# Five arms for an expert: nested comparisons become one switch with a hint, and gather, one-hot turn and add-back leave the arms

## The chip, the core and the metric

One core of one Trainium2 chip. The time is the device time of one execution in microseconds (us). TensorE is called PE, VectorE DVE, ScalarE ACT, GpSimd POOL and SyncE SP; each engine runs its own instruction stream, and semaphores order them. A "hw" matmul is one record in the trace: a float32 product of two passes shows as two.

## What is computed

Two layers of a diffusion trunk over 256 latent tokens of 1024 channels. The last part of the second layer is the one that the change touches, a SwiGLU of eight experts of which each token takes two:

```python
logits = h @ router_w + router_b
top_logit, top_idx = lax.top_k(logits, 2)
gates = einsum('btk,btke->bte', softmax(top_logit), one_hot(top_idx, 8))
for e in range(8):
    y = y + gates[..., e:e + 1] * (silu(h @ w1[e]) * (h @ w3[e])) @ w2[e]   # inner width 1408
```

The residual, a LayerNorm and the store follow.

## The kernel before

The mixers, the dense SwiGLU and the router come first; they order their instructions with a planner and by hand, and the change leaves that order as it was. Then the experts run one after the other, e = 0 to 7.

How many tokens an expert has is known only at run time. The counts are summed on TensorE (L1640), copied to int32 (`cnt`, L1644) and read into registers of PE, DVE, ACT and SP by `nc.values_load` (L1689). For each expert the function `pick` (L1934) halves the five possible arms by nested `tc.If(vals[e] > bound)` (L1940): up to 32 tokens the arm Tiny, up to 64 Small, up to 128 Full, up to 192 Full and Small, else two Fulls. Each of the four engines branches for itself. In the instruction streams the arms stand in the order Full+Full, Full+Small, Full, Small, Tiny; a comparison that holds goes on with what follows, one that doesn't jumps, and an arm ends in a jump over those behind it (Tiny, the last, has none behind it). POOL is in none of the arms.

The weights of an expert are 17 pieces of up to 1 MB; 19 slots hold them, and after its use each slot is loaded with the piece that is 19 further on (`pload`, issued by SP inside the arm).

An arm multiplies its tokens by the pieces in the order "u0 u1 u2 d0 u3 d1 u4 d2 u5 d3 t5 d4 d5" (u: up, d: down, t5: the turn of the last inner chunk). In a Full arm the weights are split on ACT (`wh`, L1286) and DVE (`wl`, L1287) into two parts that TensorE multiplies in three products (`mm3`, L248). Three further steps lie inside the arm of expert e:

- `gather` (L1656) of expert e + 1, at t5: 16 products pick its tokens with a one-hot matrix `oh` (L1663), and ACT and DVE modulate them in turn into `xg` (L1648, L1650).
- `turn_oh` (L1667), right behind it: two transposes of `oh` and a copy on ACT, kept for the way back.
- `scatter` (L1710) of expert e - 1, behind u1: four products with `yf` (L1713) and four additions on DVE into the sum (L1715).

In an arm with two blocks scatter comes first, a second one-hot and gather for the second block follow, and `turn_oh` closes the arm. `end` (Tiny: L1764, Full: L1855) leaves the expert's result in `yf`. The one-hot of expert e + 1 is made by POOL ahead of the branch (L1654).

## Time and profile before

| what | value |
|---|---|
| time, median of 3 runs | 1463.27 us (1457.28 to 1464.77) |
| the profiled execution: span from first to last instruction | 1468.2 us; no other time of it is given |
| busy: PE, weight loads, DVE, ACT, POOL | 1187.8, 895.5, 876.3, 645.8, 421.1 us |
| mean granted TensorE clock | 0.905 of full |
| HBM | 273.17 MB read, 195 GB/s over the span |

Busy times are sums over stages with different limits. The stage of the change runs from the router at 951 us to the end of the eighth expert at 1449 us.

### The profile page before, as it was taken

The page shows a single profiled execution, that of the slowest core. Times are in us where ns is not written, and L with a number is a line of the kernel's source. Part 1 is how long each engine was busy: PE and PEld are TensorE (multiplying, and loading weights), DVE is VectorE, ACT ScalarE, POOL GpSimd, SP SyncE. Part 2 cuts the span into 40 slices and gives each one's busy share as a digit, 9 for nine tenths or more (in the row PEclk, how much of TensorE's full clock was granted, in tenths as well). Part 3 has the DMA queues.
Part 4 walks back from the last instruction along what each step waited for, and adds up shares of the span by engine and source line. Part 5 has one row for each costly group of instructions (what it writes and reads, how often), then busy time and mean ns, then how long its engine had stood idle before and what let it go on. Part 6 is the DMA issues. An engine that isn't in the chain of part 4 may idle for free.

```text
span 1468.2 us, 26379 instructions
## 1 busy us (share of the span) xinstructions
PE 1187.8 (81%) x10101; PEld 895.5 (61%) x10101; DVE 876.3 (60%) x1632; ACT 645.8 (44%) x1426; POOL 421.1 (29%) x653
## 2 busy tenths in 40 slices
PE   1589679998797989878799989658978999548946
PEld 0266458776575666544698988545856556335843
DVE  7897226447566865345877785805867456113924
ACT  3433135567665766321344444214757344003810
POOL 6242122647856775501622230400000000000000
PEclk7799789999888999999899999879989999779978
DMA  8324736646555655658445555469968345589920
GB/s 342 108 79 175 224 114 205 181 122 164 141 129 117 149 147 142 133 168 337 167 170 172 175 180 202 175 243 415 370 213 289 116 150 198 205 330 412 390 83 30
DMA packets 139661, 288.59 MB, mean 197 GB/s; under 512 B 64432, under 2 KB 91184, under 8 KB 116272
## 3 DMA queue, kind: packets, MB, share of 16 engines
q1 hardware_dynamic: 136128, 278.50, 55.9%
q10 hardware_dynamic: 3312, 7.31, 1.4%
q8 instruction: 119, 1.95, 0.6%
q14 instruction: 102, 0.84, 0.2%
HBM read 273.17 MB, written 12.60 MB: 195 GB/s over the span
## 4 chain that ended last, share of the span: by engine, by line
PE 37%; issue 5%; DVE 4%; DMA 3%; ACT 1%; POOL 0%; DVEq 0%; ACTq 0%; POOLq 0%
PE pb L248 23%; PE pb L1740 3%; PE pb L1713 2%; PE pb L1663 2%; PE pb L1775 2%; DMA slot<-in_moe_w_dram 2%; DMA arena<-in_moe_w_dram 1%; PE pb L1819 1%; PE pb L1758 1%; PE pb L1789 1%; DVE wl L1287 1%; ACT wh L1286 1%; DVE usl L1435 0%; PE pb L1578 0%; DMA arena<-in_lnrows_dram 0%
## 5 line engine op out<-in xcount | busy, mean ns | idle before, releaser
L1287 DVE TENSOR_TENSOR wl<-arena,wh 128x512 fp32r<-128x512 f32 x262 | 214.5, 838 | 76.6 <-ACT wh L1286 74.4
L1286 ACT ACTIVATE wh<-arena 128x512 fp32r<-128x512 f32 x262 | 160.9, 629 | 123.4 <-PE pb L248 114.9
L1654 POOL TENSOR_SCALAR oh<-consts,consts 128x128 f32<-128x128 f32 x14 | 8.7, 633 | 381.3 <-PE pb L1758 133.5
L954 POOL TENSOR_TENSOR arena<-arena 128x126 f32<-128x126 f32 (+22 forms) x248 | 110.0, 444 | 19.4
L248 PE MATMUL pb<-usl,wh 128*128 128x256 f32 x352 | 101.5, 289 | 5.6 <-DVE usl L1435 5.6
L248 PE MATMUL pb<-ush,wh 128*128 128x256 f32 x352 | 101.6, 291 | 1.8 <-DVE fsg L1453 1.8
L248 PE MATMUL pb<-ush,wl 128*128 128x256 f32 x352 | 101.0, 288 | 0.0
L1286 ACT ACTIVATE wh<-slot 128x512 fp32r<-128x512 f32 x122 | 75.1, 629 | 39.8 <-PE pb L248 35.8
L1287 DVE TENSOR_TENSOR wl<-slot,wh 128x512 fp32r<-128x512 f32 x122 | 80.9, 688 | 18.7 <-ACT wh L1286 17.9
L266 PE MATMUL pb<-arena,sct 128*32 128x256 f32 x448 | 70.3, 424 | 23.4 <-DMA arena<-in_ada_w_dram 23.2
L1748 DVE TENSOR_TENSOR mh<-mh,pb 64x128 f32<-64x128 f32 (+1 forms) x24 | 7.0, 291 | 134.0 <-ACT mh L1747 108.7
L1317 POOL TENSOR_TENSOR arena<-arena,rows 128x2048 f32<-128x2048 f32 x11 | 51.5, 4685 | 104.9 <-DMA arena<-in_ffn_w_dram 104.9
L1099 DVE SCALAR_TENSOR_TENSOR sv<-sv,wc,pb 64x64 f32<-64x64 f32 x192 | 45.8, 278 | 57.4 <-PE pb L1083 22.2
L952 POOL TENSOR_TENSOR arena<-arena 128x126 f32<-128x126 f32 (+22 forms) x124 | 62.8, 507 | 51.3 <-DMA arena<-s 42.2
L248 PEld LDWEIGHTS pb<-usl,wh 128*128 128x128 f32 x352 | 69.2, 197 | 8.9 <-DVE usl L1435 6.5
L248 PE MATMUL pb<-wh,xsh 128*128 128x512 f32 (+1 forms) x180 | 71.7, 398 | 0.0
L248 PEld LDWEIGHTS pb<-ush,wh 128*128 128x128 f32 x352 | 68.8, 197 | 4.4 <-DVE fsg L1453 2.0
L248 PE MATMUL pb<-wl,xsh 128*128 128x512 f32 (+1 forms) x180 | 71.3, 396 | 0.0
L248 PEld LDWEIGHTS pb<-ush,wl 128*128 128x128 f32 x352 | 69.1, 197 | 1.2
L952 POOL TENSOR_TENSOR arena<-arena,X 128x126 f32<-128x126 f32 (+22 forms) x124 | 57.6, 464 | 39.4 <-DMA X<-s 30.6
L248 PE MATMUL pb<-wh,xsl 128*128 128x512 f32 (+1 forms) x180 | 67.6, 375 | 0.0
L1074 ACT ACTIVATE sv<-pb 64x128 f32<-64x128 f32 x128 | 34.6, 270 | 68.3 <-PE pb L1068 55.5
(441 smaller groups left out, 3100.9 us busy)
## 6 DMA issues: line engine op xcount, KB each, us to landing
slot<-in_moe_w_dram SPq DMA_DIRECT2D x62, 1024.0 KB, 7.9
arena<-in_moe_w_dram SPq DMA_DIRECT2D x58, 1024.0 KB, 8.0
arena<-in_ffn_w_dram SPq DMA_DIRECT2D x33, 1024.0 KB, 5.1
arena<-in_ada_w_dram SPq DMA_DIRECT2D x112, 256.0 KB, 3.1
hvr<-in_w_rkv_dram SPq DMA_DIRECT2D x12, 1024.0 KB, 5.9
wr<-in_ada_w_dram SPq DMA_DIRECT2D x10, 1024.0 KB, 6.0
sv<-v_d SPq DMA_DIRECT2D x128, 64.0 KB, 2.7
arena<-k_d SPq DMA_DIRECT2D x8, 640.0 KB, 4.0
```

The source lines that it names most:

```text
L248: i = nc.tensor.matmul(ps, lhsT=a[x], rhs=b[y], start=start and n == 0, stop=stop and n == 2)
L266: nc.tensor.matmul(ps[64 * h + 32 * g:64 * h + 32 * g + 32, 0:256], lhsT=sct[:, k], rhs=w[:, 256 * g:256 * g + 256], start=(k == 0), stop= ...
L952: eng.tensor_tensor(mv, T[:, cs, j:j + 1].to_broadcast([P, nci, nii]), X[:, ii, j].unsqueeze(1).to_broadcast([P, nci, nii]), op=ALU.mult)
L954: eng.tensor_tensor(T[:, cs, ii], T[:, cs, ii], mv, op=ALU.subtract)
L1074: nc.scalar.activation(sv_(si, d, 1)[zd(d)], PB[6][zd(d), 0:128], AF.Copy, scale=-1.0)
L1099: nc.vector.scalar_tensor_tensor(t[:, x], sv_(si, d, 0)[zd(d), x], wc_b[wc.i][zd(d), h, si:si + 1], PB[6][zd(d), 128 + 64 * h:192 + 64 * h ...
L1286: nc.scalar.activation(hi, r[:, o:o + PART], AF.Copy)
L1287: nc.vector.tensor_tensor(lo, r[:, o:o + PART], hi, op=ALU.subtract)
L1317: S.behind(nc.gpsimd.tensor_tensor(w, w, gt.unsqueeze(1).to_broadcast(w.shape), op=ALU.mult))
L1663: nc.tensor.matmul(pt[:, P * j:P * j + n], lhsT=z[:, t, P * dt:P * dt + P], rhs=oh[:, t, 0:n], start=(t == 0), stop=(t == 1))
L1713: nc.tensor.matmul(ps, lhsT=ohT[:, t], rhs=yf[:, 512 * j:512 * j + 512], start=True, stop=True)
L1740: nc.tensor.matmul(ps[32 * g:32 * g + 32, 0:P], lhsT=xg[:, k, 0:32], rhs=m[g], start=(k == 0), stop=(k == DT - 1))
```

## The change

The counts are no longer copied. Four comparisons on DVE with 32, 64, 128 and 192 add up to the number of the arm, 0 to 4, and that is loaded into the registers. `pick` and its `tc.If` are gone: `tc.Switch` jumps to one of five arms by that number, in the order Tiny, Small, Full, Full+Small, Full+Full. `tc.switch_hint` stands ahead, and the switch puts a hint for the jump at an arm's end at the start of each arm. `gather`, `turn_oh` and `scatter` stand between two switches instead of inside the arms, for experts 1 to 7 (the first gather and the last scatter lay outside the arms already). Comments and docstrings are gone too, and lines behind the top of the file move by one to seven.

```diff
+BOUNDS = (32, 64, 128, 192)
...
     cnt = c2p.tile([P, NE], I32, name="cnt")
-    S.chain(nc.vector.tensor_copy(cnt, pc[:, 0:8]))
+    armf = c2p.tile([P, NE], F32, name="armf")
+    S.chain(nc.vector.tensor_scalar(armf, pc[:, 0:8], float(BOUNDS[0]), None, op0=ALU.is_gt))
+    for i, b in enumerate(BOUNDS[1:]):
+        S.chain(nc.vector.scalar_tensor_tensor(armf if i + 2 < len(BOUNDS) else cnt, pc[:, 0:8], float(b), armf,
+                                               op0=ALU.is_gt, op1=ALU.add))
...
-    vals = [nc.values_load(cnt[0:1, e:e + 1], engines=(ENG.PE, ENG.DVE, ENG.Activation, ENG.SP), min_val=0, max_val=256)
-            for e in range(NE)]
+    ARM_ENGINES = (ENG.PE, ENG.DVE, ENG.Activation, ENG.SP)
+    vals = [nc.values_load(cnt[0:1, e:e + 1], engines=ARM_ENGINES, min_val=0, max_val=len(BOUNDS)) for e in range(NE)]
...
         if two:
-            if e > 0:
-                scatter(e - 1, ohT[(e - 1) % 2])
             onehot(e, 1, nc.vector, ohB)
...
-            if (a, c) == ("u", 1) and e > 0 and not two:
-                scatter(e - 1, ohT[(e - 1) % 2])
-            if a == "t" and not end:
-                gather(oh, xgs[0])
-                if not two:
-                    turn_oh(oh, ohT[(e + 1) % 2])
         if two:
             bl[1].end()
             scatter(e, ohT[(e + 1) % 2])
-            if not end:
-                turn_oh(oh, ohT[(e + 1) % 2])
         bl[0].end()
...
-    def pick(e, lo, hi):
...
-        m = (lo + hi) // 2
-        with tc.If(vals[e] > ARMS[m][0]) as c:
-            pick(e, m + 1, hi)
-        with c.Else():
-            pick(e, lo, m)
...
     for e in range(NE):
+
+        tc.switch_hint({g: vals[e] for g in ARM_ENGINES}, len(ARMS), f"arm{e}")
+        if e > 0:
+            gather(oh, xgs[0])
+            turn_oh(oh, ohT[e % 2])
+            scatter(e - 1, ohT[(e - 1) % 2])
         if e + 1 < NE:
             onehot(e + 1, 0, nc.gpsimd, oh)
-        pick(e, 0, len(ARMS) - 1)
+        for k in tc.Switch({g: vals[e] for g in ARM_ENGINES}, len(ARMS), hint=f"arm{e}"):
+            arm(e, ARMS[k])
```

How this stands in the built program is seen in the instruction order of two engines. First TensorE between the gather of expert 0 and its arm; TENSOR_LOAD reads a register, ISA calculates with registers. Before:

```order
L1663 MATMUL pb_64<-oh,z_8444 128x128 x7
L1663 MATMUL pb_69<-oh,z_8444 128x128 x7
L1671 MATMUL pb_70<-consts,oh 128x128
L1689 TENSOR_LOAD cnt
L1940 COMPARE_AND_BRANCH x2
```

After, with the triples of experts 2 to 6 left out:

```order
L1669 MATMUL pb_69<-oh,z_8444 128x128 x7
L1677 MATMUL pb_70<-consts,oh 128x128
L1696 TENSOR_LOAD cnt
L1936 ISA
L1936 BRANCH_PREFETCH_HINT
...
L1696 TENSOR_LOAD cnt
L1936 ISA
L1936 BRANCH_PREFETCH_HINT
L2080 SWITCH_STRIDE
L2080 ISA x2
L1943 BRANCH_PREFETCH_HINT
L1746 MATMUL pb_63<-arena,xg 32x128 x32
```

All eight register loads and all eight hints that the loop writes for the eight switches stand ahead of the first switch; DVE, ACT and SP have theirs at the same place. The hint of L1943 is the first instruction of an arm and belongs to the jump at its end. Before, each expert's load stood ahead of its own comparisons.

Second, TensorE between the last arm of expert 0 and the first of expert 1. Before, with the end of the Tiny arm, in which gather and turn stand among the last products:

```order
L1663 MATMUL pb_69<-oh,z_8444 128x128 x8
L1752 MATMUL pb_64<-consts,mh 128x32
L1663 MATMUL pb_70<-oh,z_8444 128x128 x8
L1671 MATMUL pb_63<-consts,oh 128x128 x2
L1758 MATMUL pb_65<-slot_8732,small 32x256 x8
L1758 MATMUL pb_65<-slot_8734,consts 32x256 x4
L1940 UNCONDITIONAL_BRANCH
L1689 TENSOR_LOAD cnt
L1940 COMPARE_AND_BRANCH x2
```

After, with the end of the last arm in the stream:

```order
L249 MATMUL pb_66<-wh,hh1l 128x512
L2080 UNCONDITIONAL_BRANCH
L1677 MATMUL pb_63<-consts,oh 128x128 x2
L1669 MATMUL pb_70<-oh,z_8444 128x128 x8
L1669 MATMUL pb_69<-oh,z_8444 128x128 x8
L1719 MATMUL pb_64<-yf,consts 128x512
L1719 MATMUL pb_63<-yf,consts 128x512
L1719 MATMUL pb_70<-yf,consts 128x512
L1719 MATMUL pb_69<-yf,consts 128x512
L2080 SWITCH_STRIDE
L2080 ISA x2
L1943 BRANCH_PREFETCH_HINT
```

Turn, gather and the four products of the add-back now stand in a row between the jump out of one arm and the jump into the next. DVE has the same place like this after the change:

```order
L1861 TENSOR_TENSOR yf<-pb_65,gt 128x512
L1861 TENSOR_TENSOR yf<-pb_66,gt 128x512
L2080 UNCONDITIONAL_BRANCH
L1656 TENSOR_SCALAR xg<-pb_70,raa,rab 128x128 x2
L1656 TENSOR_SCALAR xg<-pb_69,raa,rab 128x128
L1721 SCALAR_TENSOR_TENSOR x_8519<-pb_64,consts,x_8519 128x512
L1656 TENSOR_SCALAR xg<-pb_69,raa,rab 128x128
L1721 SCALAR_TENSOR_TENSOR x_8519<-pb_63,consts,x_8519 128x512
L1721 SCALAR_TENSOR_TENSOR x_8519<-pb_70,consts,x_8519 128x512
L1721 SCALAR_TENSOR_TENSOR x_8519<-pb_69,consts,x_8519 128x512
L2080 SWITCH_STRIDE
L2080 ISA x2
```

DVE reaches its own switch only behind the last of the four additions, which waits for the last product of the add-back. On all engines what stands ahead of the router and behind the last expert keeps its order.

## Rows read from the trace of the kernel before

**Rows 1.** The page's first part (busy time of each engine) and, of its second part, the granted TensorE clock in 40 slices of 36.7 us.
```profile
PE 1187.8 (81%) x10101; PEld 895.5 (61%) x10101; DVE 876.3 (60%) x1632; ACT 645.8 (44%) x1426; POOL 421.1 (29%) x653
PEclk7799789999888999999899999879989999779978
```

**Rows 2.** The waits of TensorE from 950 us to the end: which line waited, for what by the profile, us in total, times, longest. "issue" is time in which the engine waited for nothing that the profile shows.
```profile
PE pb L1740 <- issue: 54.4, 6, 17.4
PE pb L1740 <- DMA arena<-in_moe_w_dram: 20.1, 1, 20.1
PE pb L1819 <- issue: 11.2, 2, 5.7
PE pb L1819 <- DVE xsl L1804: 8.8, 1, 8.8
PE pb L1713 <- issue: 7.6, 1, 7.6
```

**Rows 3.** TensorE in the eight stretches between the last product ahead of an expert's arm and the first product in it, experts 0 to 7 in order: stretch in us, its length, PE busy (products), granted clock, mean busy share of the DMA engines, GB/s. The last row is the sum of their lengths.
```profile
960.20:974.50 14.30, 0.00 (x0) 0.68 0.53 189
1001.10:1006.50 5.40, 0.00 (x0) 0.99 1.01 405
1063.80:1072.50 8.70, 0.00 (x0) 0.73 0.35 122
1130.90:1138.40 7.50, 0.00 (x0) 0.84 0.39 142
1246.80:1264.10 17.30, 0.00 (x0) 0.65 0.18 60
1293.80:1313.70 19.90, 0.00 (x0) 0.57 0.87 338
1341.20:1346.80 5.60, 0.00 (x0) 0.78 1.02 414
1404.60:1421.40 16.80, 0.00 (x0) 0.63 0.12 37
sum 95.50, PE 0.00; mean PE 0.00
```

**Rows 4.** The line of the comparisons (L1940) on TensorE's sequencer: first all of its records, then those around each of the eight stretches of rows 3 in the same order: count, lowest, median and highest duration in ns, first and last start in us. A jump at an arm's end that is taken is recorded under the same line.
```profile
L1940 PEldq COMPARE_BRANCH  x24: 82/4705/7548, 958.0 to 1415.8; - x24
L1940 PEldq COMPARE_BRANCH  x3: 3504/5139/7548, 958.0 to 969.2; - x3
L1940 PEldq COMPARE_BRANCH  x2: 82/3057/6032, 1000.1 to 1006.2; - x2
L1940 PEldq COMPARE_BRANCH  x3: 82/4154/4796, 1062.7 to 1072.2; - x3
L1940 PEldq COMPARE_BRANCH  x3: 90/3606/4167, 1129.8 to 1134.1; - x3
L1940 PEldq COMPARE_BRANCH  x4: 4643/4780/4948, 1244.0 to 1259.1; - x4
L1940 PEldq COMPARE_BRANCH  x3: 6067/6900/7528, 1292.8 to 1306.5; - x3
L1940 PEldq COMPARE_BRANCH  x2: 82/3060/6037, 1340.2 to 1346.3; - x2
L1940 PEldq COMPARE_BRANCH  x4: 3394/4163/5287, 1403.5 to 1415.8; - x4
```

**Rows 5.** The DMA queues that carry instructions, from 1246 to 1264 us, ahead of expert 4: packets, MB, share of the 16 engines.
```profile
q8 instruction: 7, 0.11, 4.0%
q14 instruction: 12, 0.10, 1.8%
```

**Rows 6.** TensorE's products around 1340 us, at the end of expert 5 and the start of expert 6, in order of time: start, length, in brackets the idle time ahead.
```profile
1340.52 0.61 PE L1758 MATMUL pb<-arena,consts 128*32 128x256 f32 x8
1346.80 1.19 PE L1819 MATMUL pb<-arena,xg 128*128 128x512 f32 x1 [5.67 <-issue]
```

**Rows 7.** The register load (L1689) on TensorE's sequencer.
```profile
L1689 PEldq TENSOR_LOAD <-cnt x8: 303/310/498, 957.4 to 1407.5; - x8
```

**Rows 8.** Three arms: stretch, length, then busy time and count of PE, weight loads, DVE, ACT and POOL, granted clock, DMA share, GB/s. In order: expert 5 (Tiny), expert 6 (Full), expert 3 (Full and Small).
```profile
1313.70:1341.20 27.50, 27.36 (x488) 20.46 (x488) 6.39 (x14) 4.81 (x17) 0.35 (x1) 0.94 0.89 353
1346.80:1404.60 57.80, 57.73 (x259) 44.05 (x259) 50.16 (x86) 43.51 (x81) 0.00 (x0) 0.96 0.93 370
1138.40:1246.80 108.40, 108.27 (x552) 65.75 (x552) 60.29 (x102) 48.48 (x96) 1.18 (x2) 0.98 0.44 153
```

**Rows 9.** Two groups of TensorE's products in the arm of expert 5, the gather and the add-back: busy us, mean ns.
```profile
L1663 PE MATMUL pb<-oh,z 128*128 128x128 f32 x32 | 4.1, 281 | 0.0
L1713 PE MATMUL pb<-yf,consts 128*128 128x512 f32 x8 | 4.0, 618 | 0.0
```

**Rows 10.** TensorE just behind two of those stretches (experts 1 and 6) and in the arm of expert 1: stretch, length, PE busy, granted clock, DMA share, GB/s.
```profile
1006.50:1009.80 3.30, 3.27 (x4) 0.50 1.04 425
1346.80:1351.10 4.30, 4.30 (x5) 0.50 1.01 408
1012.00:1063.00 51.00, 51.00 (x249) 1.00 0.97 389
```

**Rows 11.** DVE: the end of a Tiny arm, and the four additions of one add-back; durations in ns.
```profile
L1764 DVE TENSOR_TENSOR yf<-pb,gt x4: 412/418/426, 1001.2 to 1002.5; 32x256 f32<-32x256 f32 x4
L1715 DVE SCALAR_TENSOR_TENSOR x<-pb,consts,x x4: 749/749/750, 1271.6 to 1275.3; 128x512 f32<-128x512 f32 x4
```

## The prediction, made before the changed kernel was timed

> **What bounds the kernel now.** I read the totals first, then TensorE's waits, then the stretches ahead of the arms, and last the branches in them.

> TensorE is busy 81% of the span, more than any other engine [rows 1]. That is no bound yet: the sum goes over stages. In the stage of the change its waits behind 950 us are of one kind: 54.4, 20.1, 11.2, 8.8 and 7.6 us ahead of the lines with which an expert's arm begins [rows 2]. Most carry "issue", which means that nothing the profile shows was being waited for. The two that name a DMA and DVE have the same place.

> The eight stretches between one arm's last product and the next arm's first hold no product at all and last 95.5 us together, from 5.4 us ahead of expert 1 to 19.9 us ahead of expert 5 [rows 3]. That is 6.5% of the span.

> What fills them is seen on TensorE's sequencer. Of its 24 branch records four took 0.08 to 0.09 us (the lowest in those rows where an expert's count kept the sequencer on its path); the other twenty took 3.4 to 7.5 us, about 5 us each, 100 us in all [rows 4]. Expert 5 shows it best: three jumps of 6.1, 6.9 and 7.5 us make 20.5 us, and the stretch is 19.9 us [rows 3, 4]. Each long one is a fetch of code: around expert 4, where the weights' DMA is nearly at rest, the instruction queues moved 7 and 12 packets in 18 us [rows 5]. Where weights are loading (share 0.87 to 1.02) a jump takes 6 to 7.5 us, elsewhere 3.4 to 5.3 us [rows 3, 4].

> [...]

> **The change, part by part.** The sum is made against the profiled execution, 1468.2 us; the median of the runs is 4.9 us lower, and I take that off at the end.

> *Dispatch.* Up to three comparisons become one computed jump. The trace shows no jump with a hint, so its price lies between 0.08 us (code at hand) and that of a taken jump in the same place [rows 4]. For the hints ahead of the switch I take the upper end: all eight stand ahead of the first switch, so the one for expert 7 is given some 480 us before its jump, and seven arms and their own hints come between. One jump per expert at this place's price is 5.1, 6.0, 4.8, 4.2, 4.8, 6.9, 6.0 and 4.2 us: the medians of rows 4 for experts 0, 4, 5 and 7, and the highest where one entry was taken (experts 1, 2, 3, 6). Sum 42.0 us. Around the jump two things cancel: the sequencer begins it about 1 us before the last product ends (ahead of expert 6 at 1340.2 us, product end 1341.1 [rows 4, 6]), and some 0.4 us pass from its end to the first product, plus an estimated 0.6 us for the stride and two register operations. So idle time is about the jump itself.

> *Exit.* Each arm's closing jump has its hint as the first instruction of the same arm, with nothing that replaces it in between. Here I take the lower end, 0.1 us, hidden by the same 1 us. The upper end is 3.6 to 4.8 us (the exits that are in rows 4 ahead of experts 2, 3, 4 and 7) and about 6 us where weights load.

> *Register loads.* Seven more loads at 0.31 us [rows 7] and eight times ISA and hint (estimate 0.3 us a pair) delay TensorE's first dispatch by 4.6 us, of which the gather that still runs hides about 1.2 us: +3.4 us ahead of expert 0. The other experts lose their load, 0.3 us each, inside the sequencer's lead.

> Idle ahead of the arms is then 42.0 + 3.4 = 45.4 us instead of 95.5: **50.1 us less**.

> *Moved work.* Between two arms TensorE now has turn, gather and add-back: 4.1 + 4.0 us [rows 9] and some 0.4 us for the turn, 8.5 us at seven places, 60 us. I cost this at nothing, because the arms lose the same: TensorE is busy 57.7 of 57.8 us in the Full arm and 27.4 of 27.5 in the Tiny one [rows 8], so each microsecond of products taken out shortens it. If that cover is gone, all 60 us are paid. In the Full arm the cover is thin: DVE has 50.2 us there [rows 8], less 3.0 us of additions [rows 11] and 1.6 us of gather, 45.6 us, against 57.7 - 8.5 = 49.2 us on TensorE. Between the arms the add-back waits for `yf`, four operations of 0.42 us [rows 11], which the gather covers.

> *What it costs.* DVE reaches its switch behind the fourth addition, 0.75 us after TensorE's last product, so it enters an arm about 1 us late; queued behind its jump are the low halves of the weights, for which the split products wait. The first, unsplit products of a Full arm cover that mostly; I take 1 us for each of three Full arms and 1.5 us for expert 3, whose second gather waits at once for a one-hot from DVE. Three more small DVE operations ahead of the first one-hot are 0.5 us. Together **5 us**.

> *Clock.* [...] The remaining stretches are of that length, so this largely stays; I take **3 us** back where stretches of 17 to 20 us become 5 to 7.

> Sum: 1468.2 - 50.1 + 5 - 3 = 1420 us, less 4.9: **1415 us**, its own range 1400 to 1432 us.

> **Rivals.**

> *The exits fetch too.* Then eight more jumps stand in TensorE's path: four behind arms without much loading at 4.1 us, three Tiny arms under load at 6 us, the last at 4 us, less 0.7 us of lead each: +32 us, 1447 us. For it: no row shows a hint at work, and jumps of every length in rows 4 fetch. [...] Against it: the hint stands in the arm itself.

> *The hints ahead of the switch do work,* so that the dispatches don't fetch either: 42.0 us less 8 times 0.5 are gained, and with gaps of under 1 us most of the slow starts, some 10 us: 1367 us. For it: the instructions are there. Against: their place, ahead of the first switch, all eight.

> *Slower: the moved work is added, not moved.* Place: the seven stretches between arms, where a chain gather, modulation, add-back, additions, switch now runs with nothing beside it. Price: 60 us, if something else than TensorE holds the arms at their length: DVE's splits in the Full arms, the loads (share 0.89 [rows 8]) or the fetch of code in the Tiny ones. 1415 + 60 = 1475 us. It decides once the arms give back less than a fifth of the 60 us, since the rest of the change is worth 48. Against it are the 0.1 us that TensorE rests in these arms.

> *The stretches aren't the branches'.* If a branch is worth 0.1 us and TensorE would have waited anyway, for loads or for DVE, nothing changes: about 1463 us. The row that names a DMA speaks for it, expert 4, with the DMA at 0.18 and 17.3 us all the same [rows 3], against it. [...]

> **How the numbers follow.** Chances: my forecast 0.56, exits that fetch 0.22, hints that all work 0.10, added work 0.05, stretches of another cause 0.03, something between 0.04. The time is that of the first, 1415 us. A range of 1385 to 1452 us holds it and the exits that fetch, and takes in part of the case where some dispatch hints work; 1367 and 1475 stay out. Faster by over 0.5% (below 1456 us; that is about what a measurement can tell from no change) are the first three and some of the rest, 0.91; within 0.5% 0.04; slower 0.05.

> **What would show it.** Right: one long branch record per expert and engine on TensorE, 4 to 7 us, at the switch; the exit's record short; stretches without products of 4 to 9 us; the Tiny arm near 19 us and the Full arm near 49 us of products, with 8.5 us of turn, gather and add-back ahead. Wrong: long records at the arms' ends; none at the switches; arms as long as before; or DVE's low halves as the wait of the Full arm's first split product. A loss of clock that outlasts 5 us behind each stretch would also break the sum.

## The result, and the profile after

The changed kernel takes 1423.58 us (median of 4 runs, 1419.44 to 1427.4), the kernel before beside it 1464.02 us: a ratio of 0.9743 with a 95% interval of 0.97 to 0.9787, 2.6% faster. The forecast was 1415 us with its own range of 1400 to 1432. The profiled execution has a span of 1425.4 us, where it was 1468.2.

The page of the changed kernel, busy time of each engine, answers to [rows 1]:

```profile
PE 1195.9 (84%) x10101; PEld 904.2 (63%) x10101; DVE 871.3 (61%) x1635; ACT 645.4 (45%) x1426; POOL 422.2 (30%) x653
```

The same 10101 products are done. What changed is the idle time. These are TensorE's waits from 950 us to the end in the changed kernel (line, what was waited for, us in total, times, longest), for comparison with [rows 2]. L1746 and L1825 begin an arm, L1669 is the gather, L1719 the add-back and L1677 the turn, the first work behind an arm's end:

```profile
PE pb L1746 <- issue: 23.7, 9, 5.6
PE pb L1669 <- issue: 8.3, 4, 3.6
PE pb L1825 <- DMA arena<-in_moe_w13b_dram: 5.7, 1, 5.7
PE pb L1825 <- DMA slot<-in_moe_w_dram: 5.6, 1, 5.6
PE pb L1677 <- issue: 5.2, 3, 1.8
PE pb L1719 <- ACT xg L1654: 4.7, 4, 3.7
PE pb L1669 <- DVE sct L1660: 3.6, 1, 3.6
```

The single waits of 17 to 20 us have gone, but there are new lines: before, gather and turn had no idle time of this size, and the add-back only where it began expert 3's arm. Now gather, turn and add-back lie between the arms, and so do their waits. The eight stretches ahead of the arms, with the columns of [rows 3]:

```profile
955.70:960.60 4.90, 0.03 (x5) 1.00 0.67 274
993.90:999.50 5.60, 0.01 (x1) 0.90 1.00 402
1061.10:1063.80 2.70, 0.08 (x2) 0.89 0.02 6
1125.60:1129.30 3.70, 0.07 (x2) 0.84 0.04 9
1244.60:1247.60 3.00, 0.01 (x2) 0.99 0.03 8
1281.60:1287.10 5.50, 0.00 (x0) 0.82 1.01 406
1322.30:1328.00 5.70, 0.04 (x2) 0.83 1.00 406
1386.00:1389.40 3.40, 0.04 (x5) 1.00 0.04 10
sum 34.50, PE 0.29; mean PE 0.04
```

34.5 us instead of 95.5. TensorE's jumps (line L2080 of the changed kernel), first all sixteen, then the exit of expert 0, then the dispatches of experts 4, 5 and 7; count, lowest, median and highest in ns, start in us:

```profile
L2080 PEldq COMPARE_BRANCH  x16: 307/2323/6137, 959.8 to 1406.6; - x16
L2080 PEldq COMPARE_BRANCH  x1: 2205/2205/2205, 982.8 to 982.8; - x1
L2080 PEldq COMPARE_BRANCH  x1: 3507/3507/3507, 1243.7 to 1243.7; - x1
L2080 PEldq COMPARE_BRANCH  x1: 6037/6037/6037, 1280.7 to 1280.7; - x1
L2080 PEldq COMPARE_BRANCH  x1: 3841/3841/3841, 1385.2 to 1385.2; - x1
```

The other dispatches took 0.37 (expert 0), 6.12, 3.63, 3.78 and 6.14 us (experts 1, 2, 3, 6). Queue q8, which carries instructions, starts one packet of 16384 bytes within each of the seven dispatches of 3.5 us and more, and none within the first: seven dispatches fetched and one didn't. Exits behind a lone Full arm took 0.3 us, the one behind expert 3's two blocks 0.9, those behind the Tiny arms of experts 0, 4 and 5, with the weights loading, 2.2 to 2.4, and that behind expert 7, with the loads over, 0.3.

A Tiny arm (expert 5) and a Full arm (expert 6) after, as in [rows 8] (length, busy time of PE, weight loads, DVE, ACT and POOL, clock, DMA share, GB/s):

```profile
1287.10:1311.50 24.40, 20.59 (x446) 16.19 (x446) 2.18 (x8) 2.92 (x12) 0.00 (x0) 0.90 1.02 418
1328.00:1377.80 49.80, 49.80 (x218) 38.89 (x219) 44.34 (x77) 39.55 (x73) 0.00 (x0) 0.95 0.98 381
```

**One warning on reading the times.** The part of the program ahead of the experts is the same in all kernels here, yet its length differs between the profiled executions: the router's counts begin at 951.5 us in the profiled execution of before and at 946.6 us in that of the changed kernel. (Two runs below had the same instructions and differ by 12 us there.) So beside each median the table gives the stage of the profiled execution: from the first product of the counts to the end of the span. There is one such execution of each kernel, and the two with the same instructions (x1 and x6) differ by 2.0 us in it, so a difference of that size says nothing. Before it is 1468.2 - 951.5 = 516.7 us, after 1425.4 - 946.6 = 478.8 us: 37.9 us of the 42.8 between the two spans belong to the change.

| kernel | median us | ratio to before (95%) | stage us |
|---|---|---|---|
| before | 1460 to 1464 | 1 | 516.7 |
| changed kernel | 1423.6 | 0.9743 (0.970 to 0.979) | 478.8 |
| x1 no hints ahead | 1407.8 | 0.9633 (0.960 to 0.967) | 460.4 |
| x2 hint in place | 1426.5 | 0.9770 (0.973 to 0.981) | 477.9 |
| x3 switch alone | 1413.2 | 0.9688 (0.966 to 0.972) | 467.9 |
| x4 move alone | 1472.2 | 1.0108 (1.007 to 1.015) | 521.5 |
| x5 Full first | 1413.9 | 0.9668 (0.963 to 0.970) | 475.3 |
| x6 same instructions as x1 | 1398.6 | 0.9583 (0.955 to 0.962) | 462.4 |
| x7 switch alone, no hints ahead | 1403.2 | 0.9612 (0.959 to 0.964) | 463.9 |
| x8 hints for experts 4 and 7 | 1411.8 | 0.9677 (0.965 to 0.971) | 462.3 |
| x9 changed kernel, shifted | 1406.5 | 0.9608 (0.958 to 0.964) | 461.2 |
| x10 no hints ahead, shifted | 1399.3 | 0.9577 (0.954 to 0.961) | 458.7 |
| x11 as x10, modulation on ScalarE | 1385.6 | 0.9475 (0.945 to 0.951) | 442.4 |
| x12 no hints ahead, shifted back | 1423.1 | 0.9716 (0.968 to 0.975) | 482.8 |

One of the four executions of x11, 1447.3 us at a granted clock of 0.81 where the others had 0.93 to 0.94, is a slow one and is left out of its row.

### The profile page after: what moved, and what is told of

Its sections match the earlier page's. It is cut to its first block, busy times and chain, and to the rows that moved or that the text cites. A ratio compares the mean times of both kernels' runs of the same rounds, so it can differ in the third digit from the quotient of the medians.

```text
span 1425.4 us, 26680 instructions
## 1 busy us (share of the span) xinstructions
PE 1195.9 (84%) x10101; PEld 904.2 (63%) x10101; DVE 871.3 (61%) x1635; ACT 645.4 (45%) x1426; POOL 422.2 (30%) x653
## 3 DMA queue, kind: packets, MB, share of 16 engines
q8 instruction: 97, 1.59, 0.5%
## 4 chain that ended last, share of the span: by engine, by line
PE 36%; DMA 6%; DVE 4%; issue 3%; ACT 1%; POOL 0%; DVEq 0%; SPq 0%; POOLq 0%; ACTq 0%
PE pb L249 25%; DMA arena<-in_moe_w13b_dram 3%; DMA slot<-in_moe_w_dram 3%; PE pb L1746 2%; PE pb L1781 2%; PE pb L1669 2%; PE pb L1825 1%; PE pb L1719 1%; PE pb L1795 1%; PE pb L1764 1%; DVE usl L1436 0%; PE pb L1579 0%; PE pb L1843 0%; DVE lnst L1363 0%; DVE fmk L1624 0%
## 5 line engine op out<-in xcount | busy, mean ns | idle before, releaser
L1288 DVE TENSOR_TENSOR wl<-arena,wh 128x512 fp32r<-128x512 f32 x262 | 210.8, 830 | 80.3 <-ACT wh L1287 79.5
L955 POOL TENSOR_TENSOR arena<-arena 128x126 f32<-128x126 f32 (+22 forms) x248 | 112.0, 452 | 19.4
L1288 DVE TENSOR_TENSOR wl<-slot,wh 128x512 fp32r<-128x512 f32 x122 | 79.7, 687 | 20.4 <-ACT wh L1287 19.9
L953 POOL TENSOR_TENSOR arena<-arena 128x126 f32<-128x126 f32 (+22 forms) x124 | 64.0, 516 | 47.2 <-DMA arena<-s 38.1
```

What stands on the lines that cost most here:

```text
L953: eng.tensor_tensor(mv, T[:, cs, j:j + 1].to_broadcast([P, nci, nii]), X[:, ii, j].unsqueeze(1).to_broadcast([P, nci, nii]), op=ALU.mult)
L955: eng.tensor_tensor(T[:, cs, ii], T[:, cs, ii], mv, op=ALU.subtract)
L1288: nc.vector.tensor_tensor(lo, r[:, o:o + PART], hi, op=ALU.subtract)
```

## First experiments: take the change apart

**x1, no hints ahead.**

```diff
-        tc.switch_hint({g: vals[e] for g in ARM_ENGINES}, len(ARMS), f"arm{e}")
```

> The changed kernel without the eight hints ahead of the first switch; the exits keep theirs. In the trace of the changed kernel seven dispatches on TensorE fetch (3.5 to 6.1 us) and the first takes 0.37 us. Theory: the hint that stands just ahead of the first switch covered that one, so without it expert 0's dispatch takes about 5 us and the time is 1423.6 + 4.5, less some 2 us for the instructions left out: 1426 us. Rival: the body that expert 0 takes (up to 32 tokens) is simply the next code behind the switch, so it needs no hint: the first dispatch stays at 0.4 us, the other seven as they are, and the time is 1421 to 1424 us. Either way the seven hints for later experts were worth nothing.

Measured: 1407.8 us, far below both. Expert 0's dispatch rose from 0.37 to 2.62 us, but it starts 6.0 us earlier (953.8 instead of 959.8 us), since the hints and what they calculate are gone and the register loads of the later experts now stand at their own switches. That leaves the larger part: the dispatches of experts 4, 5 and 7, all Tiny, fell from 3.5, 6.0 and 3.8 us to 0.32, 0.33 and 0.41 us, while those of experts 1, 2, 3 and 6 stayed (6.2, 4.0, 3.5, 6.1 us). It looked as if a hint did harm. That reading fell later.

**x2, the hint in its place.**

```diff
+        if e > 0:
+            nc.vector.scalar_tensor_tensor(late[e], yf[:, 0:1], 0.0, armf[:, e:e + 1], op0=ALU.mult, op1=ALU.add)
+            vals.append(nc.values_load(late[e][0:1, 0:1], engines=ARM_ENGINES, ...))
         tc.switch_hint(...)
```

> The hints ahead are moved: each expert's count is loaded and its hint given in the gap just ahead of its own switch (a small VectorE product of the last add-back's operand with zero, plus the count, makes the load wait until then). Theory of the prediction: the hints fail because all eight stand ahead of the first switch, so in their place, some 6 to 8 us ahead of the jump, they cover most of the fetch: TensorE's dispatch records of experts 1 to 7 fall from 33.1 us together to 3 to 14 us, and the time from 1423.6 to 1397 to 1407 us. Rival: a hint in the same stretch of code as its jump is not used (VectorE's and ScalarE's exits behind short or half-long arms fetch although hinted), so the records stay at 3.5 to 6.1 us and the loads add some 3 us: 1424 to 1430 us.

Measured: 1426.5 us, the rival. On TensorE the hint of expert 1 is given at 987.2 us and the jump begins 5.0 us later; it still takes 5.73 us, against 6.12 us in the changed kernel:

```profile
L2083 PEldq COMPARE_BRANCH  x1: 5730/5730/5730, 992.2 to 992.2; - x1
```

All seven dispatches stayed between 3.4 and 6.4 us. The hints of experts 2 to 7 stood only 2.2 to 2.7 us ahead of their jumps, less than the 6 to 8 us that were meant. Even so a hint that worked should have taken that much off, and the dispatches of experts 2, 3 and 6 took 3.4, 3.7 and 6.2 us where they had taken 3.6, 3.8 and 6.1. A hint ahead of a switch, far ahead or up to 5 us ahead, saved nothing on TensorE that shows here.

**x3, the switch alone, and x4, the move alone.** In x3 the lines that the diff takes out of `arm` are put back, and the three calls ahead of the switch are gone; in x4 `pick` and `tc.If` are back.

> The switch with its hints, but gather, one-hot turn and add-back stay inside the arms as before: the switch alone. Theory: outside the arms the moved work costs 12 us more than the prediction's 5 (a wait of TensorE for ScalarE's modulation behind VectorE's late exit, two fetches of the code behind the arms, three exits under load), which go again; each gap between arms is one dispatch of 4 to 6 us: about 1411 us. Rival 1: those waits move into the gaps instead (VectorE, late at the exit, is late by a dispatch more at the next arm): 1420 to 1430 us. Rival 2: without work between arms the hint at an arm's start and the exit stand as before, but the exits' fetch now shows ahead of each dispatch: 16 jumps fetch, 1440 to 1447 us.

> The nested comparisons of the kernel before, but with gather, one-hot turn and add-back outside the arms: the move alone. Theory: the comparisons stay at their 100 us on TensorE, so the kernel stays near 1464 us and the move adds 5 to 15 us: 1469 to 1479 us. Rival: the moved work stands beside the fetches of VectorE and ScalarE and shortens the code between branches, so that the move gains on its own: 1445 to 1460 us.

Measured: x3 1413.2 us (stage 467.9), the first theory; x4 1472.2 us (stage 521.5), the first theory too. So the switch alone is worth 48.8 us of the stage (516.7 - 467.9), and the move costs 10.9 us on top of the switch (478.8 - 467.9). By itself it costs 4.8 us in the stage (521.5 - 516.7), but the profiled execution of x4 was the fastest of its six; by the medians, 1472.2 against 1459.9 us, it costs 12.3, and no trace shows where its slower runs lose their time. In x3 every dispatch but the first fetched, 4.1 to 7.3 us, and every exit took 0.3 to 1.0 us.

## Second experiments: what makes a dispatch short

**x5, another order of the bodies**, without hints ahead.

```diff
-    ARMS = [[Tiny], [Small], [Full], [Full, Small], [Full, Full]]
+    ARMS = [[Full], [Small], [Tiny], [Full, Small], [Full, Full]]
```

> No hints ahead (as in the run without them), and the order of the five bodies is Full, Small, Tiny, Full+Small, Full+Full instead of Tiny, Small, Full, ...; the comparisons are changed to match. Theory: TensorE loads code in sequence, so a dispatch is short when the body taken is the one that stands next behind the switch, and a fetch for any other. Then the short records change hands: experts 1, 2 and 6 (Full) fall from 6.2, 4.0 and 6.1 us to 0.3 to 2.6 us, experts 4, 5 and 7 (Tiny) rise from 0.3 to 0.4 us to 3.5 to 6.5 us, expert 0 from 2.6 to about 5 us; time 1402 to 1412 us, about that of the run without hints. Rival: Tiny is short for another reason (a short body, an arm taken before and still loaded): the records stay with Tiny, experts 1, 2 and 6 stay at 4 to 6 us.

Measured: half of it. The Tiny dispatches rose to 6.1, 4.0, 6.1 and 3.4 us (experts 0, 4, 5, 7), as the theory has it. Of the Full ones only expert 6's fell; those of experts 1 and 2 stayed at 6.1 and 3.4 us. Expert 6:

```profile
L2080 PEldq COMPARE_BRANCH  x1: 423/423/423, 1315.7 to 1315.7; - x1
```

Behind a switch no body but the first was entered in less than 3.4 us in any of these runs; being the first isn't enough.

**x6** was to leave out the hints at the arms' ends as well, by leaving out the switch's `hint=`.

> No hints ahead and none at the arms' ends. Theory of the prediction: the exits' hints cover the fetch behind an arm (0.3 us after a Full arm); without them the four exits behind Full and Full+Small arms take 3.5 to 6.5 us each on TensorE and those behind Tiny arms too instead of 2.2: 20 to 28 us more than the 1407.8 us of the run without hints ahead, 1428 to 1436 us. Rival: the code behind an arm is reached without a fetch anyway, or the hints hurt here as they do ahead: 1400 to 1410 us.

That argument only names the jump: the built program has the same instructions as x1 on all engines (26488 records in both traces), and the exits' hints are still in the trace. So what the exits' hints are worth stays open. As a second run of x1's instructions it was useful: the jumps agree (0.40, 0.42 and 0.32 us for experts 4, 5 and 7), the stage is 462.4 and 460.4 us, while the medians, 1398.6 and 1407.8 us, differ by 9. The difference lies ahead of the stage. First product of the counts in x1, then in x6:

```profile
946.43 0.61 PE L1638 MATMUL pb<-sel,consts 128*128 128x16 f32 x2 [12.52 <-DVE sel L1635]
```

```profile
934.09 0.61 PE L1638 MATMUL pb<-sel,consts 128*128 128x16 f32 x2 [9.29 <-DVE sel L1635]
```

**x7, the switch alone without hints ahead** (x3 and x1 together).

> The switch alone (gather, turn and add-back inside the arms) and no hints ahead: the two gains together. Theory, that they add: of the 1413.2 us of the switch alone go the dispatches into the Tiny body of experts 4, 5 and 7 (4.1, 5.5 and 4.3 us to 0.4 each) and 4.6 us of loads' and hints' time ahead of expert 0, whose dispatch rises by 2.3 us: 1398 to 1401 us. Rival: without work between the exit and the next dispatch the code in sequence is not there in time, so that the Tiny dispatches stay at 4 to 6 us: 1410 to 1414 us.

Measured: 1403.2 us (stage 463.9). By the jumps the rival is right: the Tiny dispatches of experts 4, 5 and 7 took 3.8, 5.2 and 4.3 us, without any hint ahead. Only the 4.0 us of the loads and hints ahead of expert 0 came; the other 6 us between the medians lie ahead of the stage. Where the dispatch follows 1.0 to 1.4 us behind the exit, even the jump into the first body is long.

**x8, hints ahead for experts 4 and 7 alone.**

```diff
+        if e in (4, 7):
             tc.switch_hint({g: vals[e] for g in ARM_ENGINES}, len(ARMS), f"arm{e}")
```

> The changed kernel with only the hints ahead for experts 4 and 7, both still ahead of the first switch. Expert 5, also Tiny, has none. Theory 1, a hinted jump fetches by itself: the dispatches of experts 4 and 7 take 3.5 to 6 us, that of expert 5 takes 0.3 to 0.5 us; time 1407.8 + 7 + 1 = 1413 to 1418 us. Theory 2, a hint that is still pending spoils all jumps behind it: experts 4, 5 and 7 all take 3.5 to 6.5 us, 1418 to 1424 us. Theory 3, only the last hint given counts: expert 4 short or long, 5 short, 7 long.

Measured: expert 4 (hinted) 3.41 us, expert 5 (not hinted) 0.41, expert 7 (hinted) 0.41; 1411.8 us. All three theories fall: by the first and the third expert 7 would be long, by the second experts 5 and 7. Expert 0's jump took 0.36 us here with no hint of its own, against 1.9 to 2.6 us in x1, x6 and x7, so its own hint isn't what made it short either; what did was not tested. So I looked for what moves with the number of hints and not with the hints themselves: the place of the code.

## The border between two packets of code

In the Tiny arm of expert 5 after the change TensorE stops twice for nothing that the profile shows. From the timeline (start, length, in brackets the idle time ahead), with what lies between the stops:

```profile
1298.90 0.85 PE L1746 MATMUL pb<-slot,xg 128*32 128x128 f32 x22 [1.19 <-issue]
1299.69 0.27 PE L1758 MATMUL pb<-consts,mh 64*128 64x64 f32 x1
1299.89 1.07 PE L1764 MATMUL pb<-slot,consts 128*32 128x256 f32 x16
1300.78 1.93 PE L1746 MATMUL pb<-arena,xg 128*32 128x128 f32 x64
1302.64 0.27 PE L1758 MATMUL pb<-consts,mh 64*128 64x64 f32 x1
1302.84 1.07 PE L1764 MATMUL pb<-arena,small 128*32 128x256 f32 x16
1303.73 0.60 PE L1746 MATMUL pb<-arena,xg 128*32 128x128 f32 x6
1305.99 1.69 PE L1746 MATMUL pb<-arena,xg 128*32 128x128 f32 x26 [1.67 <-issue]
```

22 + 1 + 16 + 64 + 1 + 16 + 6 = 126 products of two instructions each (weight load and matmul), with 4 semaphore records between them 256 instructions from stop to stop. In the same arm the instruction queue whose packets fall into TensorE's long jumps moved

```profile
q8 instruction: 4, 0.07, 1.1%
```

4 packets, 0.07 MB; over the whole execution it moved 97 packets of 16384 bytes, 1.59 MB. One of them starts at 1296.3 us and the next at 1303.4, each 2.6 us ahead of the end of a stop. So one packet comes to 256 instructions, 64 bytes each (an estimate from these two numbers), and a stop marks the border between two. The same stop is seen in the code between the arms. The gap ahead of expert 4 in the changed kernel:

```profile
1232.10 2.17 PE L1669 MATMUL pb<-oh,z 128*128 128x128 f32 x18
1237.63 3.29 PE L1669 MATMUL pb<-oh,z 128*128 128x128 f32 x14 [3.36 <-issue]
1240.76 3.80 PE L1719 MATMUL pb<-yf,consts 128*128 128x512 f32 x8
1247.59 1.72 PE L1746 MATMUL pb<-slot,xg 128*32 128x128 f32 x28 [3.03 <-issue]
```

A border lies behind the 18th product of the gather, and the dispatch behind it fetches again. The border comes later with each expert: behind products 8, 18 and 24 of the gather ahead of experts 3, 4 and 5, as the timeline has it, steps of 20 and 12 instructions; carried on like this (an estimate, no stop shows it) it lies near the gather's end and in the add-back for experts 6 and 7. From expert 3 on it is, by these steps, always inside the some 89 instructions between two arms. Without hints ahead (x1) it lies at product 21 ahead of expert 1 (stop of 3.0 us there) and, by the same steps, behind the switch from expert 4 on. With two hints (x8) the first stop is at product 14, and by the steps the border is behind the switch from expert 5 on. That fits every dispatch of experts 1 to 7 into the first body in x1, x5 and x8: short where no border lies between exit and switch, long where one does. Three runs tested it, with products put into an arm that isn't taken here (expert 0, two Fulls), so that only the place of the later code changes:

```diff
             turn_oh(ohB, ohT[(e + 1) % 2])
+            if e == 0 and kinds[1] is Full:
+                for _ in range(34):
+                    nc.tensor.matmul(PB[gen.ids[gen.n % len(gen.ids)]][:, 0:P], lhsT=ident, rhs=ident)
```

**x9**, the changed kernel with all its hints and 34 such products:

> The changed kernel with all its hints; the only edit puts 34 products (136 of TensorE's instructions) into the Full+Full arm of expert 0, which is never taken here, so nothing more is executed and only the place of the later code moves. In the traces TensorE's code comes in packets of 16384 bytes, and the fetches fall 256 instructions apart. In the changed kernel such a border lies inside the some 89 instructions between two arms at product 10, 20 and 26 of the gather ahead of experts 3, 4 and 5, and by the same step of about 15 instructions an expert at some 67 and 79 for experts 6 and 7; in the run without hints ahead it lies behind the switch from expert 4 on. Theory, the border decides and not the hint: moved by 120 instructions the border lies behind the switch for all seven, the stops of 3.4 to 3.6 us inside the gathers of experts 3 and 4 go, and the dispatches of experts 4, 5 and 7 (3.5, 6.0, 3.8 us) fall to 0.3 to 0.5 us: 18 to 20 us less, 1402 to 1408 us. Rival, the hints ahead do the harm: dispatches stay at 3.5 to 6 us, 1416 to 1424 us.

Measured: 1406.5 us, stage 461.2 (478.8 before the shift). The dispatches of experts 4, 5 and 7 took 0.41, 0.43 and 0.41 us. First that of expert 5, then the gap ahead of expert 4:

```profile
L2083 PEldq COMPARE_BRANCH  x1: 427/427/427, 1272.4 to 1272.4; - x1
```

```profile
1234.36 3.74 PE L1669 MATMUL pb<-oh,z 128*128 128x128 f32 x32
1237.93 3.80 PE L1719 MATMUL pb<-yf,consts 128*128 128x512 f32 x8
1241.66 1.61 PE L1746 MATMUL pb<-slot,xg 128*32 128x128 f32 x49
```

The gather runs through its 32 products, and the arm follows with no pause above 0.1 us.

**x12**, no hints ahead and 16 such products, the other way:

> No hints ahead, and 16 such products (64 instructions) in the arm that is never taken: the border moves to where it lies in the changed kernel, inside the code between the arms ahead of experts 3 to 7. Theory, the border decides: the dispatches of experts 4, 5 and 7 rise from 0.3 to 0.4 us to 3.5 to 6.2 us without any hint, and the gathers stop again; some 15 us more than the run without hints ahead, from the first product of the routing to the end 473 to 478 us instead of 460; 1414 to 1424 us. Rival, the hints did it: the dispatches stay at 0.3 to 0.4 us, 460 us.

Measured: 1423.1 us, stage 482.8 (460.4 and 462.4 before the shift), some 21 us where 15 were expected. Against x1, 15 us of the difference are idle time of TensorE, as expected; the other 7 are slower products (busy 405.7 us in the stage against 398.5, at granted clocks of 0.91 and 0.94). The gap ahead of expert 4 stops at product 17, and the dispatches of experts 4, 5 and 7 took 3.7, 6.0 and 3.8 us with no hint ahead of any switch:

```profile
1228.44 2.06 PE L1669 MATMUL pb<-oh,z 128*128 128x128 f32 x17
1233.27 1.94 PE L1669 MATMUL pb<-oh,z 128*128 128x128 f32 x15 [2.76 <-issue]
1235.05 3.80 PE L1719 MATMUL pb<-yf,consts 128*128 128x512 f32 x8
1242.48 1.93 PE L1746 MATMUL pb<-slot,xg 128*32 128x128 f32 x32 [3.63 <-issue]
```

x9 and x12 settle it: it was the place of the code and not the hints. The hints ahead cost their own time ahead of expert 0, and by chance moved the code to a bad place. That it is the border that matters about the place is the account that fits every such jump; two things it leaves open. A dispatch fetches behind a border although the body it enters stands only some tens of instructions further on. And inside the Tiny arms the stops don't move with the code: in the changed kernel they stand behind products 252 and 378, that is 512 and 768 records behind the jump, for experts 0, 4 and 5 alike (not each shows in each arm), and in x6, with no hints ahead of expert 0, its arm stopped behind products 125 and 251. There the stops go with the arm's start.

**x10**, no hints ahead and 43 products, and **x11**, the same with all the modulation on ScalarE:

```diff
-        if dt % 2:
+        if True:
             nc.scalar.activation(dst, src, AF.Identity, scale=r_a[:, dt:dt + 1], bias=r_b[:, dt:dt + 1])
```

> No hints ahead, and 43 such products (172 instructions) in the arm that is never taken, so that the border lies behind the switch ahead of all experts, also of 1 and 2, where it lies at instructions 48 and 66 in the run without hints ahead. Theory: the stops inside those gathers (3.0 and 1.2 us) go, the dispatches of experts 4, 5 and 7 stay at 0.3 to 0.5 us, those of 1, 2, 3 and 6 (not the first body) stay at 3.4 to 6.2 us; from the first product of the routing to the end some 3 to 5 us less than the 460 us there; 1396 to 1404 us. Rival: the stops come from VectorE's late exit and stay: 460 us.

> As the run before it (no hints ahead, 43 products), and all of the gathered rows' modulation on ScalarE, which leaves the long arms in 0.4 to 1.1 us, where VectorE takes 5.5 to 6.4 us behind a Full arm. Theory: TensorE's waits for the modulated rows' bank ahead of the add-back (2.0, 3.4 and 2.0 us ahead of experts 2, 3 and 7) go: 5 to 7 us less than the run before it, 1390 to 1398 us. Rival: eight modulations on one engine take as long as the wait (8 times some 0.4 us), or the add-back waits for VectorE's last operation on its operand anyway: no change.

Measured: x10 1399.3 us, stage 458.7, 1.7 to 3.7 us less than x1 and x6, which is no clear gain where these two differ by 2.0. The stops inside the gathers of experts 1 and 2 are gone, but ahead of expert 2 the add-back then waits longer for the modulated rows, 4.06 us where it was 2.04. x11 1385.6 us, stage 442.4: 16.3 us less than x10, where 5 to 7 were expected, and the fastest of all, 5.2% below the kernel before. TensorE behind the Full arm of expert 1 in x10:

```profile
1039.60 3.74 PE L1669 MATMUL pb<-oh,z 128*128 128x128 f32 x32
1043.17 1.02 PE L1719 MATMUL pb<-yf,consts 128*128 128x512 f32 x2
1048.25 4.40 PE L1719 MATMUL pb<-yf,consts 128*128 128x512 f32 x6 [4.06 <-ACT xg L1654]
```

and in x11:

```profile
1040.68 3.74 PE L1669 MATMUL pb<-oh,z 128*128 128x128 f32 x32
1044.25 3.60 PE L1719 MATMUL pb<-yf,consts 128*128 128x512 f32 x8
```

The waits of 4.1, 2.9 and 2.2 us (experts 2, 3 and 7) are gone, 9.1 us. The expectation left out the rest: six products after the wait took 4.40 us, at a granted clock of 0.63, eight without it 3.60 at 1.00, and the additions on DVE no longer stand between modulations. The seven stretches from exit to dispatch are 59.0 us instead of 73.7 on TensorE's sequencer, which is 14.7 of the 16.3.

## Why the prediction was right, point by point

The time came within 8.6 us, and the main mechanism is shown: the branches' fetches were the empty stretches, and the switch without the move (x3) takes 48.8 us out of the stage. The prediction had 50.1 from the branches and 48.1 in all. The changed kernel got 37.9 in its stage. Another 4.9 us came ahead of the stage, by no part of the change, and made the agreement closer than it was earned.

**Dispatch, 42.0 us.** Measured 33.4 us (0.37, 6.12, 3.63, 3.78, 3.51, 6.04, 6.14, 3.84). Seven of eight terms are right to 1.3 us, each a taken jump at its place's price; for the three Tiny ones (experts 4, 5 and 7) that was luck: they cost it only where the code happened to lie, and in x9 the same jumps took 0.4 us. (The prediction's split of the prices by load, 6 to 7.5 us with the weights loading and 3.4 to 5.3 elsewhere, leaves out the 7.5 us ahead of expert 0 at a share of 0.53 [rows 3, 4].) The first, 5.1 us, was wrong: 0.37. That the hints ahead wouldn't work is borne out by x2, but the reason given, that all eight stand too early, isn't: one given 5 us ahead did no better. And the step missed that a jump into the first body can be short: 0.3 to 0.4 us for experts 4, 5 and 7 in x1 and x9, where the same jumps took 3.5 to 6.0 us behind a border. The prediction gave every jump the price of a taken one. (Its estimate of 0.6 us for the stride and two register operations was high: from the first of them to the jump pass 0.2 us, 959.6 to 959.8 us ahead of expert 0.)

**Register loads and hints, 3.4 us.** 4.87 us idle ahead of expert 0, of which 0.4 is the jump: 4.5 us, 1.1 more than forecast. The 0.3 us for ISA and hint was an estimate that no row shows. The eight loads start 0.81 us apart on average (953.2 to 958.9 us), each 0.30 us long at the median, which leaves 0.5 us for ISA and hint.

**Exits, 0.1 us each.** Right on TensorE behind lone Full arms (0.31 to 0.34 us), wrong behind the three Tiny arms under load: 2.2 to 2.4 us, 5.2 us of idle time together. The load alone isn't the cause: in x3 and x7, with the moved work in the arms and the same loads, these three exits took 0.3 to 0.4 us. And the step looked at TensorE alone. DVE's exit from a Full arm shows like this ahead of expert 2 (TensorE, DVE and ACT in order of time):

```profile
1049.54 1.29 DVE L1861 TENSOR_TENSOR yf<-pb,gt 128x512 f32<-128x512 f32 x2 [0.70 <-PE pb L249]
1053.59 1.02 PE L1719 MATMUL pb<-yf,consts 128*128 128x512 f32 x2
1056.40 0.41 DVE L1656 TENSOR_SCALAR xg<-pb,raa,rab 128x128 f32<-128x128 f32 x1 [5.57 <-issue]
1056.85 0.46 ACT L1654 ACTIVATE xg<-pb,rab,raa 128x128 f32<-128x128 f32 x1 [6.24 <-DVE xg L1656]
1058.29 2.84 PE L1719 MATMUL pb<-yf,consts 128*128 128x512 f32 x6 [3.68 <-ACT xg L1654]
```

DVE stands 5.57 us and waits for nothing that the profile shows, which points to its own code; ACT waits for DVE, and TensorE's add-back for a bank that both have to empty. x11 takes this away.

**Moved work at nothing, and 5 us of cost.** The arms gave back what the moved work takes: from first to last product the eight arms are 337.7 us together where they were 392.2, 54.5 less; the prediction's 60 - 5 is 55. That the sums agree is in part luck: expert 5 gave back 3.6 us where 8.5 were taken out of it, expert 7 9.4 where only the add-back's 4.0 were. The Full arm kept its forecast (49.8 against 49) and the Tiny one of expert 5 did not: 24.4 us instead of near 19 (expert 7's, with the loads over, took 18.0). Its products fell from 27.36 to 20.59 us, and two stops at borders, 1.19 and 1.67 us, appeared in an arm that had rested 0.1 us [rows 8].

**What was missing.** Between the arms, the seven stretches from last to first product take 109.0 us: 62.0 of work and 47.0 of idle time. The prediction had 60 and 36.9. The dispatches in it are 29.4, 7.5 less than forecast, and 17.6 us were not in the sum: 5.2 of exits, 8.0 of stops at borders inside the gathers (3.58, 3.36 and 1.08) and 4.4 of waits for the modulated rows (3.68 and 0.68). That the code between the arms can itself be late was no rival; it is the step that was mis-sized. New waits for the modulated rows take back part of what a shifted border gives (3.98 and 3.67 us ahead of experts 2 and 3 in x9).

**Clock, -3 us.** No run shows this term. Behind the stretch ahead of expert 6 TensorE has half its clock for as long as in [rows 10], and so it has for 3.3 us behind the one ahead of expert 1:

```profile
1328.00:1332.30 4.30, 4.30 (x5) 0.50 1.03 410
```

and for the same 3289 products of the stage its busy time rose from 399.7 to 402.1 us. (The rest of the rise from 1187.8 to 1195.9 us lies ahead of the stage.)

**The rivals.** That the exits fetch too was true in part (TensorE behind Tiny arms, 2.2 to 2.4 us, and DVE behind Full ones, by the 5.57 us above). That hints ahead do all the work was refuted by x2 and by x9, in which the long jumps of experts 1, 2, 3 and 6 stay at 3.6 to 6.3 us. That the move costs was true at 4.8 to 12.3 us alone (x4) and 10.9 us on the switch, not at 60. That the stretches weren't the branches' was refuted by x3.

## What to carry to other kernels

Where control flow lies on the path, count instructions: the code between a jump out and the next jump in should hold no border between packets of code (17.6 us of the stage in x9), and the body taken most often should stand first behind the switch (0.3 to 0.4 us in x1 and x9, where other bodies took 3.5 us and more); here padding an arm that isn't taken placed the rest at no cost that shows. Ask of every engine, not only of the busiest, when it is through its jump, and give what follows to the one that is through first. And compare stages, not whole times, when programs differ in a part that is not under test.
